# Gate and up products in two halves of the channels, in a layer with 32 experts

## The chip, the core and the metric

The kernel runs on one core of a Trainium2 chip. The metric is device time in microseconds (us), from three runs. The core's engines are TensorE (PE in the profile, PEld its weight loads), VectorE (DVE), ScalarE (ACT), GpSimd (POOL) and SyncE (SP), which here issues the weights' transfers.

## What is computed

One decoder block over 512 tokens of 1024 channels: a mixer (recurrent channels and windowed attention), then a mixture of 32 experts, in which each token goes to 4. The change touches the experts alone:

```
gu   = xb @ w_gu[e] + b_gu[e]                 # 1024 -> 2048
gate = minimum(gu[:, :1024], 7);  up = clip(gu[:, 1024:], -7, 7)
y    = ((up + 1) * gate * sigmoid(1.702 * gate)) @ w_down[e] + b_down[e]
out += router weight * y                       # rows of the tokens of expert e
```

With these inputs the experts get 48, 18, 90, 113, 36, 43, 293, 33, 22, 97, 64, 10, 23, 125, 10, 25, 113, 121, 13, 104, 39, 19, 3, 100, 68, 3, 42, 136, 69, 58, 17 and 93 rows (experts 0 to 31).

## The kernel before, in words

**Weights.** All is float32. An expert has eight chunks of gate and up weights (128 channels x 2048, 1 MB each) and four of down weights (1 MB). SyncE loads them in the order of use into a ring of 20 slots (`ORDER`, L1099). `pump` (L1129) issues loads as long as slots are free in program order; `paced` (L1105) makes SyncE read a word of the fourth load before, so that at most four are under way. `used` (L1134) gives back the slots of an expert's gate and up weights behind `gate_up`, those of its down weights behind `down`. A load into such a slot waits on the chip until TensorE has passed the last product that reads it, and with it the end of the nest of branches.

**Tiles.** The rows of an expert are taken in tiles of 32, up to four (a block of 128). `gu` (L1191) makes one tile's gate and up products: for each of 8 chunks (`k`) four products of 128x32 by 128x512, side by side in four column groups of the array, added up in one PSUM bank (`pg`, L1138). `act` (L1200) adds the bias and makes the activation: seven VectorE instructions and one on ScalarE, the result turned into `H[e % 2]`. `dn` (L1214) makes the tile's down products into half a bank (`pd`, L1140), and `put` (L1221) scales them on VectorE and adds them to their tokens' rows in HBM by an indirect DMA of GpSimd.

**Branches.** The tiles 1 to 3 stand in a nest of branches on the row count (`nest`, L1167): each engine falls through into a tile that exists, and jumps out behind the last one. `hint` tells an engine ahead of a tile whether the branch behind it will be taken. Experts with over 128 rows (6 and 27) run `further` (L1259) inside the innermost branch: blocks 1 to 3, each with gather, transposes, all products and sums. Its code stands in the instruction streams for every expert.

**Order.** One pass of the loop (L1303) for expert e: `gate_up(e)`, where two steps that prepare the row lists of expert e+2 (`prep`, `where`, `spots`) stand between pieces of tile 0; slots back; bias and transposes of the rows of expert e+1 (`turn_x`, `scale_x`) into the one buffer `xT`; the gather of the rows of e+2; `down(e-1)`; slots back. PSUM in this order: gate tiles 0 to 3 in banks 0 to 3, down tiles in banks 4 and 5 by turns, the transposes in 6 and 7, the lists in 5. In `further`: transposes in 0 and 1, gate tiles in 2 and 3, down tiles in 0 and 1. Block 1's rows are gathered into `XR` at the start of the pass (`second_rows`); the rows of block 2 and its lists ahead of block 1's products (L1272 to L1276).

Of the kernel before, what the change touches and what calls it, by code (L numbers as in the profile page):

```python
# [22 lines left out]
KD = 8  # L23
# [17 lines left out]
def block_kernel(ctx, tc, x, c, w_ada, b_ada, g_mix, w_in, conv_w, conv_b, w_rg_a, b_rg_a, w_rg_x,  # L41
# [16 lines left out]
    pall = psp.tile([128, 8, 512], FT, name="pall")  # L58
# [14 lines left out]
    class Carve:  # L73
# [3 lines left out]
        def tile(self, shape, dt, name=None, **kw):  # L77
            n = 1
            for d in shape[1:]:
                n *= d  # L80
            w = n if dt != BF else n // 2
            v = self.t[:shape[0], self.o:self.o + w]
            self.o += (w + 7) // 8 * 8
            assert self.o <= 2048, name
            v = v if dt == FT else v.bitcast(dt)
            if len(shape) == 3:
                v = v.rearrange("p (a b) -> p a b", a=shape[1])
            if len(shape) == 4:
                v = v.rearrange("p (a b c) -> p a b c", a=shape[1], b=shape[2])
            return v  # L90
# [639 lines left out]
    def run_all(g):  # L730
        for _ in g:
            pass
# [309 lines left out]
    def prep(e, c, oh, own=None, bk=5, tbs=range(NT)):  # L1042
        mk = (lambda n: own[n]) if own else new
        for tb in tbs:
            hot(oh, e, c, tb)
        yield
        where(e, c, oh, mk, bk)
        yield
        yield from spots(e, c, mk)
# [30 lines left out]
    def gather(e, b, x_, reg=None):  # L1080
        XROW[e, b] = x_

        def rows(p0, p1):
            G.indirect_dma_start(out=x_[p0:p1], out_offset=None, in_=h2_d,  # L1084
                                 in_offset=bass.IndirectOffsetOnAxis(
                                     ap=GI[e, b // 2][p0:p1, b % 2:b % 2 + 1], axis=0),
                                 bounds_check=S - 1, oob_is_err=False)

        if reg is None:
            return rows(0, 128)  # L1090
        with tc.If(reg > 128 * b + 64) as cmp:  # L1091
            rows(0, 128)
        with cmp.Else():
            with tc.If(reg > 128 * b + 32) as small:
                rows(0, 64)
            with small.Else():
                rows(0, 32)
# [33 lines left out]
            load(*todo.pop(0))  # L1131
            n = n and n - 1

    def used(e, down):  # L1134
        free.extend(HELD.pop((e, down)))
        pump()

    pg = lambda b, t: pall[:, 2 + t % 2 if b else t, :]  # L1138

    pd = lambda b, t: pall[:, (0 if b else 4) + t % 2, 0:256]  # L1140


    def xpose(e, b, xT):
        turn_x(e, b, xT)
        scale_x(e, b, xT, 0, 4)

    def scale_x(e, b, xT, k0, k1):
        p = pall[:, 0 if b else 6, :].rearrange("p (k n) -> p k n", k=4)
        for k in range(k0, k1):
            A.activation(xT[:, k, :], p[:, k, :], AF.Identity, scale=g2c[:, k:k + 1], bias=sh2c[:, k:k + 1])  # L1150

    def turn_x(e, b, xT):
        x_ = XROW[e, b]
        for q in range(2):
            p = pall[:, (0 if b else 6) + q, :].rearrange("p (k n) -> p k n", k=4)
            for i in range(4):
                k = 4 * q + i
                PE.transpose(p[:, i, :], x_[:, k * 128:(k + 1) * 128], ident)  # L1158
            if q:
                ks = slice(4, 8)  # L1160
                V.tensor_tensor(xT[:, ks, :], p, g2c[:, ks, None].to_broadcast([128, 4, 128]), op=OP.mult)
                V.tensor_tensor(xT[:, ks, :], xT[:, ks, :], sh2c[:, ks, None].to_broadcast([128, 4, 128]),
                                op=OP.add)
        XT[e, b] = xT


    def nest(r, b, body, after=None, mark=None):  # L1167
        with branch(r, 128 * b + 32, mark, 1):  # L1168
            hint(r, 128 * b + 64, mark, 2)
            body(1)  # L1170
            with branch(r, 128 * b + 64, mark, 2):  # L1171
                hint(r, 128 * b + 96, mark, 3)
                body(2)
                with branch(r, 128 * b + 96, mark, 3):
                    hint(r, 128 * b + 128, mark, 4, after)
                    body(3)
                    if after:
                        with branch(r, 128 * b + 128, mark, 4):
                            after()
# [7 lines left out]
    def hint(r, n, mark, i, there=True):  # L1187
        if mark and there:
            tc.mark_branch_hint_location(f"{mark}_{i}", hint=r > n, engines=WORKERS)

    def gu(e, b, t, k0=0, k1=KD):  # L1191
        xT, w = XT[e, b], WG[e]
        for k in range(k0, k1):
            for j in range(4):
                PE.matmul(pg(b, t)[32 * j:32 * j + 32], xT[:, k, 32 * t:32 * t + 32], w[k][:, j],  # L1195
                          start=(k == 0), stop=(k == KD - 1), tile_position=(0, 32 * j))
# [3 lines left out]
    def act(e, b, h, t):  # L1200
        p = pg(b, t)
        ga, up, sg, hr = (TU[:, i] for i in range(4))
        V.tensor_tensor(ga, p[:, 0:256], BG[:, 0:256], op=OP.add)  # L1203
        V.tensor_tensor(up, p[:, 256:512], BG[:, 256:512], op=OP.add)  # L1204
        V.tensor_scalar(ga, ga, 7.0, None, op0=OP.min)  # L1205
        A.activation(sg, ga, AF.Sigmoid, scale=1.702)  # L1206
        V.tensor_scalar(up, up, -7.0, 7.0, op0=OP.max, op1=OP.min)
        V.tensor_tensor(ga, ga, sg, op=OP.mult)  # L1208
        by_k = lambda v: v.rearrange("p (i k) -> p i k", k=KD)
        V.scalar_tensor_tensor(hr.rearrange("p (k i) -> p i k", k=KD), by_k(up), 1.0, by_k(ga),  # L1210
                               op0=OP.add, op1=OP.mult)
        V.transpose(h[:, t], hr)  # L1212
# [18 lines left out]


    H = [part(0), part(2)]
    TU, Y, HX, XR, bdx = part(1), part(3), part(4), a4[5], a4[6][:, :256]

    def gate_up(e, r, between):
        def tile(t):
            gu(e, 0, t)
            act(e, 0, H[e % 2], t)

        ks = (0, 2, 6, 8) if e else (0, 7, 8, 8)
        hint(r, 32, f"g{e}", 1)
        for i in range(3):
            gu(e, 0, 0, ks[i], ks[i + 1])
            if i < 2:
                between()
        act(e, 0, H[e % 2], 0)
        nest(r, 0, tile, lambda: further(e, r), f"g{e}")

    def down(e, r):  # L1250
        def tile(t):
# [7 lines left out]
    def further(e, r):  # L1259
        own = {n: new(n, n + "x") for n in ("g1", "i1", "gi", "f", "si")}  # L1260

        def products(t):
            gu(e, b, t)
            act(e, b, HX, t)

        def sums(t):
            dn(e, b, HX, t)
            put(e, b, t)

        def block():  # L1270
            xpose(e, b, XT[e, 0])
            if b < 3:  # L1272
                with tc.If(r > 128 * b + 128):
                    if b == 1:
                        run_all(prep(e, 1, T_HOT, own, 1))
                    gather(e, b + 1, XR)  # L1276
            products(0)
            nest(r, b, products)
            sums(0)
            nest(r, b, sums)  # L1280

        bias2(e, bdx)
        b = 1
        block()
        with tc.If(r > 256):
            b = 2
            block()
            with tc.If(r > 384):
                b = 3
                block()  # L1290

    pump(KD + 4 + EARLY)
# [10 lines left out]
    for e in range(NE):  # L1303
        r = rn
        if e:
            second_rows(e)
            bias2(e - 1)
        prs = [prep(e + 2, 0, T_HOT)] if e + 2 < NE else []
        if e == 0:
            prs = [prep(u, 0, OH[u], None, bk, ()) for u, bk in ((1, 5), (0, 7), (2, 4))]  # L1310
        for pr in prs:
            next(pr)
        if e == 0:
            gates_of()

        def between():
            for pr in prs:
                next(pr, None)
            if e == 0 and (1, 0) not in XROW:
                gather(1, 0, xg)  # L1320
                second_rows(0)

                nc.sync.value_load(xg.bitcast(I32)[0:1, 0:1])
                pump()

        gate_up(e, r, between)
        used(e, False)
        if e:
            hint(rp, 32, f"d{e - 1}", 1)
        for pr in prs:  # L1330
            run_all(pr)
        if e + 1 < NE:
            rn = count(e + 1)
            bias(e + 1)
            turn_x(e + 1, 0, new("xT"))
            scale_x(e + 1, 0, XT[e + 1, 0], 0, 4)
        if e + 2 < NE:
            gather(e + 2, 0, xg, G.value_load(cnt[0:1, e + 2:e + 3], min_val=0, max_val=S))  # L1338
        if e:
            down(e - 1, rp)  # L1340
            used(e - 1, True)
        rp = r
# [59 lines left out]
```

## Time and profile before

| | us |
|---|---|
| median of 3 runs | 1525.4 (1521.98 to 1530.1) |
| profiled execution | 1519.37 |
| its span, first to last instruction | 1517.5 |
| TensorE products, busy | 1226.6 |
| VectorE, ScalarE, GpSimd busy | 617.5, 210.3, 264.1 |
| mean granted clock of TensorE | 0.926 |

The span has a mixer part of some 250 us, the stage of the experts from about 257 to 1494 us, and a last norm. Products of 128x32 by 128x512 (L1195) run four at a time in the column groups, so a sum of their durations says nothing; a stretch in the timeline with its count does. In rows of waits, "<-" names what ended the wait, a small q behind an engine (PEq L1178) its sequencer: there, the exit of the nest at that line (L1168 behind one tile, L1171 two, L1174 three, L1178 four). L1288 and L1285 are the exits of `further`.

### The profile page before, as it was taken

How to read it: one execution, taken by the hardware profiler on the slowest of the kernel's cores; microseconds unless marked ns; L12 is line 12 of the kernel's file. 1: busy time of each engine (PE TensorE's matmuls, PEld its weight loads, DVE VectorE, ACT ScalarE, POOL GpSimd, SP SyncE). 2: the span in 40 equal slices, each digit the busy share in tenths (PEclk: the TensorE clock that was granted, in tenths of full speed). 3: DMA queues.
4: the chain of work that ended last, by engine and by line, in shares of the span. 5: the costliest groups of instructions: out<-in, count | busy, mean ns of one | idle time of the engine just before them, and what ended most of it. 6: DMA issues, size and time to landing. Idle time of an engine off the chain costs nothing. (4 is left out here: it accounts for less than half of the span.)

```text
span 1517.5 us, 32068 instructions
## 1 busy us (share of the span) xinstructions
PE 1226.6 (81%) x12297; PEld 541.8 (36%) x12297; DVE 617.5 (41%) x1687; ACT 210.3 (14%) x467; POOL 264.1 (17%) x224
## 2 busy tenths in 40 slices
PE   6998979678888988789777688798858887879782
PEld 4655657222332433223212322352412242233331
DVE  4738856424344333333323323433422343324323
ACT  3445524100100010000000000000000000000001
POOL 3305731100120012101100200110200031011102
PEclk9998999999999999989878988999978999999997
DMA  9973158897996039989998988897998899579963
GB/s 325 334 281 102 56 233 327 352 379 306 399 388 250 10 88 406 384 337 400 391 398 330 395 360 339 310 388 305 398 394 311 364 392 405 209 286 347 401 263 124
DMA packets 94319, 473.02 MB, mean 312 GB/s; under 512 B 12888, under 2 KB 36652, under 8 KB 42764
## 3 DMA queue, kind: packets, MB, share of 16 engines
q1 hardware_dynamic: 76684, 447.39, 74.5%
q0 software_dynamic: 16928, 20.21, 6.0%
q8 instruction: 176, 2.88, 0.8%
q14 instruction: 179, 1.47, 0.2%
q10 hardware_dynamic: 352, 1.07, 0.2%
HBM read 457.78 MB, written 17.06 MB: 313 GB/s over the span
## 5 line engine op out<-in xcount | busy, mean ns | idle before, releaser
L1195 PE MATMUL pall<-wc,xT 128*32 128x512 f32 x5248 | 643.0, 635 | 131.2 <-DMA wc<-in_w_gu_dram 64.4
L1195 PEld LDWEIGHTS pall<-wc,xT 128*32 128x32 f32 x5248 | 166.3, 114 | 526.1 <-issue 414.4
L1218 PE MATMUL pall<-wc,a 128*32 128x256 f32 x5248 | 306.2, 389 | 34.2 <-DVE a L1224 19.1
L1218 PEld LDWEIGHTS pall<-wc,a 128*32 128x32 f32 x5248 | 176.0, 112 | 157.5 <-issue 29.4
L1226 POOL DMA_INDIRECT x_d<-a,si x82 | 128.2, 1563 | 409.7 <-DVE a L1225 259.0
L1206 ACT ACTIVATE a<-a 128x256 f32<-128x256 f32 x82 | 34.2, 417 | 916.0 <-DVE a L1205 916.0
L1203 DVE TENSOR_TENSOR a<-pall,bg 128x256 f32<-128x256 f32 x82 | 34.8, 425 | 275.7 <-PE pall L1195 275.7
L1084 POOL DMA_INDIRECT xg<-h_d,gi x31 | 33.0, 1064 | 634.2 <-PE pall L1158 486.5
L1158 PE MATMUL pall<-ident,xg 128*128 128x128 f32 x248 | 37.7, 301 | 53.8 <-PEq L1168 23.4
L1150 ACT ACTIVATE xT<-pall,sh2c,g2c 128x128 f32<-128x128 f32 x136 | 51.2, 456 | 214.4 <-DVEq L1171 55.4
L1224 DVE TENSOR_TENSOR a<-pall,bd 128x256 f32<-128x256 f32 x75 | 31.7, 422 | 100.8 <-PE pall L1218 95.2
L928 DVE LOAD_MASK_SELECT bg<-btg x32 | 0.4, 14 | 155.2 <-DVEq L1171 48.5
L1056 DVE COPY f<-pall 128x8 f32<-128x8 f32 x33 | 5.5, 167 | 139.3 <-PE pall L1053 139.2
L1158 PEld LDWEIGHTS pall<-ident,xg 128*128 128x128 f32 x248 | 30.2, 154 | 81.1 <-issue 81.1
L1210 DVE SCALAR_TENSOR_TENSOR a<-a 128x256 f32<-128x256 f32 x82 | 50.1, 611 | 2.8
L233 PE MATMUL pall<-hp,wp 128*128 128x512 f32 x112 | 47.3, 422 | 2.3 <-ACT hp L287 1.7
L1208 DVE TENSOR_TENSOR a<-a 128x256 f32<-128x256 f32 x82 | 34.9, 426 | 27.9 <-ACT a L1206 23.5
L234 PE MATMUL pall<-hp,wp 128*128 128x512 f32 x112 | 45.3, 405 | 0.5 <-DVE hp L289 0.5
L235 PE MATMUL pall<-hp,wp 128*128 128x512 f32 x112 | 45.0, 402 | 0.0
L1225 DVE SCALAR_TENSOR_TENSOR a<-a,f,gt 128x256 f32<-128x256 f32 x82 | 39.7, 485 | 2.9
L1212 DVE STREAM_TRANSPOSE a<-a 128x256 f32<-128x256 f32 x82 | 36.5, 445 | 2.8
L1204 DVE TENSOR_TENSOR a<-pall,bg 128x256 f32<-128x256 f32 x82 | 34.0, 415 | 0.0
(295 smaller groups left out, 1015.3 us busy)
## 6 DMA issues: line engine op xcount, KB each, us to landing
wc<-in_w_gu_dram SPq DMA_DIRECT2D x256, 1024.0 KB, 11.1
wc<-in_w_down_dram SPq DMA_DIRECT2D x128, 1024.0 KB, 11.3
wc<-in_w_ada_dram SPq DMA_DIRECT2D x24, 1024.0 KB, 8.6
wc<-in_w_in_dram SPq DMA_DIRECT2D x7, 1024.0 KB, 11.9
a<-in_x_dram SPq DMA_DIRECT2D x4, 512.0 KB, 4.5
wc<-in_w_out_dram SPq DMA_DIRECT2D x4, 512.0 KB, 6.7
wc<-in_w_out_dram SPq DMA_DIRECT2D x2, 1024.0 KB, 4.8
out_dram<-wc SPq DMA_DIRECT2D x4, 512.0 KB, 2.7
```

What stands on the lines that cost most here:

```text
L233: PE.matmul(out, ah, bh, start=start, stop=False)
L234: PE.matmul(out, ah, bl, start=False, stop=False)
L235: PE.matmul(out, al, bh, start=False, stop=stop)
L1150: A.activation(xT[:, k, :], p[:, k, :], AF.Identity, scale=g2c[:, k:k + 1], bias=sh2c[:, k:k + 1])
L1158: PE.transpose(p[:, i, :], x_[:, k * 128:(k + 1) * 128], ident)
L1195: PE.matmul(pg(b, t)[32 * j:32 * j + 32], xT[:, k, 32 * t:32 * t + 32], w[k][:, j], start=(k == 0), stop=(k == KD - 1), tile_position=(0, ...
L1208: V.tensor_tensor(ga, ga, sg, op=OP.mult)
L1210: V.scalar_tensor_tensor(hr.rearrange("p (k i) -> p i k", k=KD), by_k(up), 1.0, by_k(ga), op0=OP.add, op1=OP.mult)
L1212: V.transpose(h[:, t], hr)
L1218: PE.matmul(pd(b, t)[32 * j:32 * j + 32], ht[:, t, 32 * k:32 * k + 32], w[k][:, j], start=(k == 0), stop=(k == KD - 1), tile_position=(0, ...
L1225: V.scalar_tensor_tensor(y, y, f[:, 1, b % 2, t:t + 1], gt2, op0=OP.mult, op1=OP.mult)
L1226: st = G.indirect_dma_start(out=x1_d, out_offset=bass.IndirectOffsetOnAxis(ap=si[:, b % 2, t:t + 1], axis=0), in_=y, in_offset=None, bound ...
```

## The change

`gate_up` runs the channels 0 to 511 (chunks 0 to 3) of all tiles first, in a nest of its own, then `further`, gives back the first four slots, and runs chunks 4 to 7 and the activation of all tiles in a second nest, whose exits have hints of their own; then the other four slots go back. The lists stand behind chunks 1 and 3 of tile 0. In `further` the banks are others, `xT` of the first block stays whole (`xt2` takes the turned rows of further blocks), `HX` and `XR` are one buffer, and the lists and the gather of block 2 (and the gather of block 3) stand behind the block before. The down products of the first block use banks 4 to 7.

```diff
-    def used(e, down):
-        free.extend(HELD.pop((e, down)))
+    def used(e, down, n=4):
+        free.extend(HELD[e, down][:n])
+        del HELD[e, down][:n]
         pump()
-    pg = lambda b, t: pall[:, 2 + t % 2 if b else t, :]
-    pd = lambda b, t: pall[:, (0 if b else 4) + t % 2, 0:256]
+    pg = lambda b, t: pall[:, 6 + t % 2 if b else t, :]
+    pd = lambda b, t: pall[:, 4 + (t % 2 if b else t), 0:256]
...
     def scale_x(e, b, xT, k0, k1):
-        p = pall[:, 0 if b else 6, :].rearrange("p (k n) -> p k n", k=4)
+        p = pall[:, 4 if b else 6, :].rearrange("p (k n) -> p k n", k=4)
...
-            p = pall[:, (0 if b else 6) + q, :].rearrange("p (k n) -> p k n", k=4)
+            p = pall[:, (4 if b else 6) + q, :].rearrange("p (k n) -> p k n", k=4)
...
-    TU, Y, HX, XR, bdx = part(1), part(3), part(4), a4[5], a4[6][:, :256]
+    TU, Y, HX, XR, bdx = part(1), part(3), part(5), a4[5], a4[6][:, :256]
+    xt2 = a4[4].rearrange("p (k n) -> p k n", k=KD)
     def gate_up(e, r, between):
+        hint(r, 32, f"g{e}", 1)
+        gu(e, 0, 0, 0, 2 if e else 4)
+        between()
+        gu(e, 0, 0, 2 if e else 4, 4)
+        between()
+        nest(r, 0, lambda t: gu(e, 0, t, 0, 4), lambda: further(e, r), f"g{e}")
+        used(e, False, 4)
+        hint(r, 32, f"h{e}", 1)
         def tile(t):
-            gu(e, 0, t)
+            gu(e, 0, t, 4, KD)
             act(e, 0, H[e % 2], t)
-        ks = (0, 2, 6, 8) if e else (0, 7, 8, 8)
-        hint(r, 32, f"g{e}", 1)
-        for i in range(3):
-            gu(e, 0, 0, ks[i], ks[i + 1])
-            if i < 2:
-                between()
-        act(e, 0, H[e % 2], 0)
-        nest(r, 0, tile, lambda: further(e, r), f"g{e}")
+        tile(0)
+        nest(r, 0, tile, None, f"h{e}")
+        used(e, False, 4)
...
         def block():
-            xpose(e, b, XT[e, 0])
-            if b < 3:
-                with tc.If(r > 128 * b + 128):
-                    if b == 1:
-                        run_all(prep(e, 1, T_HOT, own, 1))
-                    gather(e, b + 1, XR)
+            xpose(e, b, xt2)
             products(0)
...
         with tc.If(r > 256):
+            run_all(prep(e, 1, T_HOT, own, 4))
             b = 2
+            gather(e, b, XR)
             block()
...
         gate_up(e, r, between)
-        used(e, False)
```

## Rows read from the trace of the kernel before

**Rows 1.** The page of the profile: busy time of the engines, and the transfers' busy share in 40 slices of the span.
```profile
PE 1226.6 (81%) x12297; PEld 541.8 (36%) x12297; DVE 617.5 (41%) x1687; ACT 210.3 (14%) x467; POOL 264.1 (17%) x224
...
DMA  9973158897996039989998988897998899579963
```
**Rows 2.** The table by stretch: start and end us, us; busy us of TensorE, its weight loads, VectorE, ScalarE and GpSimd (instructions); granted clock; the transfers' share and GB/s.
```profile
1035.00:1174.00 139.00, 105.28 (x1092) 38.28 (x1090) 46.11 (x144) 9.24 (x24) 16.62 (x12) 0.89 0.96 376
...
1338.00:1475.00 137.00, 115.16 (x1330) 47.72 (x1330) 44.38 (x125) 9.36 (x24) 20.59 (x14) 0.95 0.93 358
```
**Rows 3.** SyncE's waits over the span: who waits, for what; us in total, times, longest.
```profile
SPq L1119 <- PEq L1288: 85.1, 1, 85.1
SPq L1119 <- PEq L1178: 74.7, 7, 13.5
SPq L1119 <- PEq L1285: 30.5, 1, 30.5
SPq L1119 <- PEq L1174: 21.8, 3, 8.8
```
**Rows 4.** The timeline of SyncE: start us, us from the first to the end of the last, what is issued, how many.
```profile
465.73 97.84 SPq L1119 DMA_DIRECT2D wc<-in_w_gu_dram  x8
...
1262.61 20.97 SPq L1119 DMA_DIRECT2D wc<-in_w_gu_dram  x8
...
1296.73 43.51 SPq L1119 DMA_DIRECT2D wc<-in_w_gu_dram  x8
```
**Rows 5.** TensorE's waits from 257 to 1494 us, columns as in group 3.
```profile
PE pall L1195 <- DMA wc<-in_w_gu_dram: 64.4, 45, 9.5
PE pall L1158 <- PEq L1168: 23.4, 11, 5.3
PE pall L1195 <- ACT xT L1150: 22.0, 6, 7.5
PE pall L1218 <- DVE a L1224: 19.1, 9, 2.4
PE pall L1195 <- PEq L1171: 13.5, 4, 4.5
...
PE pall L1158 <- PEq L1171: 8.7, 8, 1.7
PE pall L1158 <- PEq L1178: 7.3, 7, 1.1
...
PE pall L1158 <- PEq L1285: 6.2, 1, 6.2
PE pall L1158 <- PEq L1288: 5.2, 1, 5.2
...
PE pall L1158 <- PEq L1174: 3.1, 3, 1.0
```
**Rows 6.** The timeline of TensorE: start us, us, line, what it writes and reads, shapes, instructions (64 make a tile), and in brackets the wait before. The first row is gate tiles without a wait, the second two down tiles.
```profile
462.00 21.66 PE L1195 MATMUL pall<-wc,xT 128*32 128x512 f32 x200 [0.68 <-DMA wc<-in_w_gu_dram]
...
549.39 7.11 PE L1218 MATMUL pall<-wc,a 128*32 128x256 f32 x128 [0.45 <-PEq L1171]
```
**Rows 7.** The table by stretch, columns as in group 2, around four holes of the weight stream.
```profile
1020.00:1037.00 17.00, 15.98 (x164) 5.54 (x156) 7.92 (x21) 1.25 (x3) 0.87 (x1) 1.00 0.46 172
...
1303.00:1340.00 37.00, 26.77 (x272) 9.91 (x264) 13.57 (x36) 3.49 (x10) 1.57 (x1) 0.96 0.27 99
939.00:956.00 17.00, 16.12 (x152) 4.68 (x144) 6.07 (x17) 0.83 (x2) 0.00 (x0) 1.00 0.42 176
475.00:562.00 87.00, 76.56 (x879) 30.51 (x872) 32.32 (x88) 6.23 (x16) 10.44 (x7) 0.94 0.14 31
```
**Rows 8.** VectorE's waits over the span, for its own sequencer at the exit of the gate nest, ahead of the next expert's bias; columns as in group 3.
```profile
DVE bg L928 <- DVEq L1171: 48.5, 8, 6.4
DVE bg L928 <- DVEq L1178: 42.0, 7, 6.8
DVE bg L928 <- DVEq L1168: 41.0, 11, 5.8
DVE bg L928 <- DVEq L1174: 17.9, 3, 6.0
```
**Rows 9.** The timeline of VectorE: first and last of the seven instructions of one tile's activation.
```profile
374.91 0.42 DVE L1203 TENSOR_TENSOR a<-pall,bg 128x256 f32<-128x256 f32 x1 [3.82 <-PE pall L1195]
...
377.54 0.45 DVE L1212 STREAM_TRANSPOSE a<-a 128x256 f32<-128x256 f32 x1
```
**Rows 10.** Expert 6: the timeline of TensorE, block 1's transposes and its first products; that of GpSimd, the gather of block 2; and of the page's kind of list of DMA issues the row of such gathers (how many, median us from issue to landing).
```profile
483.60 1.09 PE L1158 MATMUL pall<-ident,small 128*128 128x128 f32 x8
...
490.48 29.52 PE L1195 MATMUL pall<-wc,xT 128*32 128x512 f32 x256 [0.16 <-issue]
...
490.74 1.04 POOL L1084 DMA_INDIRECT small<-h_d,gi  x1 [33.98 <-DVE f L1056]
...
xg<-h_d,gi POOLq DMA_INDIRECT x31, 8.1
```
**Rows 11.** The timeline of TensorE behind a wait (expert 10, tile 0), and the table by stretch for the time after it.
```profile
675.99 3.64 PE L1195 MATMUL pall<-wc,xT 128*32 128x512 f32 x16 [3.19 <-ACT xT L1150]
...
676.00:686.00 10.00, 9.43 (x52) 2.38 (x56) 4.53 (x15) 0.99 (x3) 1.57 (x1) 0.53 1.02 411
```

More of the change, by code (lines that the diff above doesn't have):

```diff
@@ L1289, in further @@
                 b = 3
+                gather(e, b, XR)
                 block()
```

## The prediction

> **What bounds the kernel now.** I read the page first. TensorE is busy for 81% of the span and the transfers' share by slices swings between 9 and 0 [rows 1], so neither limit holds throughout. The table by stretch says more: from 1035 to 1174 us the transfers run at a share of 0.96, from 1338 to 1475 at 0.93 [rows 2]. The expert stage therefore alternates: the weight stream is full for a while, then it stops, then TensorE waits for it. Why it stops is in SyncE's waits: 85.1 us in one wait for the exit of expert 6's further blocks, 30.5 us for expert 27's, and 74.7 and 21.8 us in ten waits for the exits of four- and three-tile experts [rows 3]. The ring has 20 one-megabyte slots. While expert e's gate and up products run, 12 are held and 8 can be filled; the next slots come free only behind the last tile. The timeline of SyncE shows the two largest holes: eight gate and up loads take 21.0 us to issue from 1262.61 us on, where none waits for a slot, but 97.8 us from 465.73 on and 43.5 from 1296.73 on [rows 4]. TensorE's waits show the other side: 64.4 us for gate and up weights, 22.0 for the turned rows xT, 19.1 for a bank that VectorE has not yet read, and 42.5 us (23.4 + 8.7 + 7.3 + 3.1) in 29 exits from the gate nest [rows 5].
>
> **Part 1, the split.** Multiplications, weight loads and bytes stay as they are. A gate tile costs 21.66 / 200 x 64 = 6.93 us, so a half 3.5 us; a down tile 7.11 / 2 = 3.56 us [rows 6]. New is that four slots come free after the first halves of all tiles, for a four-tile expert 13.9 us before the old point. The longest of the seven waits at such exits is 13.5 us [rows 3], so they nearly vanish; the four remaining slots follow 14 us later, about when four loads have landed. On SyncE the four loads move ahead of four others; behind them stand only loads, and nothing else uses that queue in this stage. Tile 0 now needs four chunks before the other tiles have work, not eight, so a starved start covers itself: three more half tiles (10.4 us) run while chunks 4 to 7 land. Of the 64.4 us of weight waits I take 40 as removed; the ends are 20 (the stream as late as now) and 64.
>
> How much room the stream has: its idle time is 17 x 0.58 = 10 us at 939 to 956, 17 x 0.54 = 9 at 1020 to 1037, 37 x 0.73 = 27 at 1303 to 1340, and 87 x 0.86 = 75 at 475 to 562 [rows 7]. The first two can go; of the third about 14 (half of four gate tiles earlier); of the fourth about 4, worked out in part 3; some 10 from smaller holes. Room: 47 us. A gain beyond that is not to be had from this edit.
>
> **Part 2, the exits.** Each nest is left by a jump. Today the gate nest's exit jumps over `further` as well, and costs TensorE 1.0 us where the hint stands a whole tile (7 us) ahead (7.3 / 7, 8.7 / 8, 3.1 / 3) but 5.2 and 6.2 us at the two exits of `further`, which have no hint [rows 5]. After the change the far jump closes the first half, with its hint only half a tile, 3.5 us, ahead. Bounds: 1.0 us each if the hint still suffices, 5.24 if it does nothing. Taken off 5.24, a lead of 3.5 us leaves 1.7; I take 2.0, nearer the lower row because that row's hint works the same way with a longer lead. For 30 experts (6 and 27 keep their price): 60 us. The second half gets an exit too, a short jump: 23 experts x 0.9 = 21 us, between 0 and the 3.4 us of 13.5 / 4, which are waits at short exits of the down nest [rows 5]; seven four-tile experts fall through. Against these stand the 42.5 us of today's exits. The net is +39.
>
> The Trainium skill, "Runtime: NRT & Kernel Launch", section "Instruction fetch mechanics", says that a taken branch to a target outside the fetched window stalls the engine until the target's page has come, and mentions no hint. The trace agrees for the two unhinted exits (5.2 and 6.2 us) and not for the hinted ones (1.0); by the rule alone the 60 us would be 157. What that does is the first rival.
>
> VectorE pays more at this exit: its bias shuffle waits 48.5 / 8 = 6.1, 42.0 / 7 = 6.0, 41.0 / 11 = 3.7 and 17.9 / 3 = 6.0 us behind it [rows 8]. Its part of a tile, 374.91 to 377.99, is 3.1 us [rows 9], less than the new 3.5 us per half tile, so it doesn't fall behind. VectorE meets the far jump while TensorE is still in the first halves, where it has nothing to do; from the second half it leaves by a short one. With two or more tiles the 6 us are hidden; with one tile VectorE starts its activation some 2 us late and then saves the jump, about even. So the turned rows of the next expert come some 4 us sooner after a large expert: four waits of 3.2 us, 13 of the 22.0. If the short jump stalls VectorE too, this is 0.
>
> **Part 3, banks and further blocks.** Four banks for down products, with VectorE no longer 6 us late, remove the 19.1 us. Banks 6 and 7 also hold the turned rows of the next expert; ScalarE and VectorE read them before down tile 2 comes, 7 us after the transposes. If VectorE is late as now, about half comes back (bounds 0 and 19).
>
> In expert 6 the lists and the gather of block 2 now stand after block 1 (XR and HX share a buffer). GpSimd's gather waits for the last reader of HX; behind it stand only block 2's scatters, and TensorE's transposes wait for it. Today the lists already cost TensorE the time from 484.69 to 490.48 us, 5.8 us, and the gather (1.04 us to issue, 8.1 to land) hides under block 1 [rows 10]. Then 9.1 us lie bare, bounds 5 and 20. The pause also lets the clock fall: after a wait of 3.19 us at 675.99 the next 10 us had 0.53 of the clock [rows 11], so I add 3.5. First release of slots for expert 6: half of four gate tiles (13.9 us) earlier, 9.1 later, so about 4 us sooner: that is the 4 above. Expert 27 has one block more than its first and no such gather.
>
> **The sum** on TensorE, against the profiled execution (span 1517.5, 1519.4 us in all): -40 -13 -19 +39 +9 +3.5 = -20.5. The stream has room for 47, so it permits that. Profiled time: 1499. The median of the runs, 1525.4, lies 6 us above the profiled one; against it I forecast 1504 us.
>
> **Rivals.**
> First, *the far jump decides, slower*. Place: TensorE's exit from the first half, 30 times. Price: 5.24 instead of 2.0, 97 us; pauses above 3 us also bring the low clock, as at 675.99 [rows 11], on perhaps ten of the 21 experts with several tiles, 3 us each. Against my 20.5 that is +107 if all lands on the path. It doesn't: with one tile the weight stream is the limit and covers it, so 21 x 3.2 + 30 - 20.5 = +77 at most. It decides from about 3 us per exit (21 x 1 us takes back my 20.5). For it: one-tile exits cost 2.1 us on average with a lead of a whole tile and up to 5.3 [rows 5], so hints fail at times. Against: all 18 hinted exits with two to four tiles cost about 1.0. All failing would give 1602. I take half as failing: 10.5 x 3.2 + 15 - 20.5 = +28, so 1553.
>
> Second, *the stream is the limit anyway, no change*. At shares of 0.96 [rows 2] earlier slots are filled no faster, the holes move to expert 6 and 27, and the rest eats what is left: 14 + 4 us at these two, less 3.5 of clock and about 10 of exits in large experts. Time: 1521. Against: the holes at 939 and 1020 us are of the kind that the earlier release ends.
>
> Third, *the exits stay at 1.0 us*, hints sufficing: another 30 us, held by the room of 47: 1480.
>
> Fourth, *VectorE's stall follows to the second exit*, so that the parts about turned rows and banks bring nothing: -20.5 + 13 + 10, 1528.
>
> **How the numbers follow.** A difference below 0.5%, 7.6 us, can't be told from none in this kernel. Forecast's own case 0.46 and range 1490 to 1516; third rival 0.10; first rival 0.28; second and fourth 0.16, of which a little falls on the faster side. Faster 0.57, same 0.15, slower 0.28. The range takes in the third rival and the first as far as half its exits failing: 1480 to 1552.
>
> **What would show it.** Right: SyncE's waits at exits of four-tile experts fall from 74.7 us to under 20, expert 6's wait stays above 70; TensorE's wait for gate and up weights about halves; its wait for VectorE's bank reads is gone; VectorE's 6 us waits move from the bias shuffle to the exit of the first half; TensorE shows 30 waits of about 2 us there; in expert 6 a pause of 12 to 18 us ahead of block 2. Wrong: waits of 3 us and more at the first exit in most experts with several tiles, with more stretches at the low clock; or the stream's holes at the old places.

## The result, and the profile after

| | us |
|---|---|
| before, median of 19 runs | 1524.57 |
| changed, median of 19 runs | 1536.28 (1528.72 to 1538.47) |
| ratio, 95% interval | 1.0068 [1.0053, 1.0084] |
| profiled execution, span | 1533.51, 1531.6 |

The change made the kernel slower by 0.7%. The prediction, 1504 us, had the sign wrong. Lines moved in the file: L1196 is the gate product (L1195 before), L1219 the down product, L1159 the transposes; nests are left at L1169 (one tile), L1172 (two), L1175 (three) and L1179 (four). L1292 and L1287 are the exits of `further`.

TensorE's waits from 257 to 1510 us in the changed kernel (who waits, for what; us in total, times, longest):
```profile
PE pall L1196 <- PEq L1169: 68.8, 15, 5.8
PE pall L1196 <- PEq L1172: 31.4, 11, 5.3
PE pall L1196 <- issue: 22.7, 10, 7.5
...
PE pall L1196 <- PEq L1179: 12.1, 7, 4.0
PE pall L1196 <- DMA wc<-in_w_gu_dram: 10.0, 2, 5.1
...
PE pall L1196 <- DMA wc<-in_w_down_dram: 8.2, 3, 2.8
...
PE pall L1196 <- ACT xT L1151: 1.2, 1, 1.2
...
PE pall L1219 <- DVE a L1225: 0.5, 1, 0.5
```
Against [rows 5], what was to go went, and more than was forecast: 64.4 us for weights are 10.0, 22.0 for turned rows are 1.2, 19.1 for banks 0.5. In its place stands TensorE's own sequencer, ahead of gate products. The timeline of expert 18 (one tile, no weights late) shows where: the first half ends at 995.3, the second begins at 1000.5.
```profile
993.41 1.92 PE L1196 MATMUL pall<-wc,xT 128*32 128x512 f32 x16
995.27 0.19 PE L1053 MATMUL pall<-g,rep 128*128 128x40 bf16 x1
1000.51 5.91 PE L1196 MATMUL pall<-wc,xT 128*32 128x512 f32 x32 [5.04 <-PEq L1169]
```
The second half then takes 5.91 us for 32 instructions where half a gate tile takes 3.5 [rows 6]: part of the pause is paid again in clock, of which 0.61 was granted there (the third figure from the end; columns as in [rows 2]):
```profile
1000.50:1006.40 5.90, 5.89 (x32) 1.35 (x32) 0.00 (x0) 0.00 (x0) 0.00 (x0) 0.61 0.98 378
```
VectorE's bias waits behind the exit, 149.4 us in [rows 8], are gone, as forecast:
```profile
DVE bg L928 <- DVEq L1169: 8.0, 11, 0.8
DVE bg L928 <- DVEq L1172: 7.5, 8, 1.0
...
DVE bg L928 <- DVEq L1175: 2.8, 3, 1.0
```
SyncE's waits for slots did not shrink but spread; at the exits of four-tile experts (L1179) 36.6 us are left of 74.7, where the prediction wanted under 20. They are no holes that starve anyone (TensorE's weight waits say so): SyncE waits for slots that a late TensorE still holds.
```profile
SPq L1119 <- PEq L1292: 86.8, 1, 86.8
SPq L1119 <- PEq L1172: 58.2, 11, 8.8
SPq L1123 <- PE pall L1196: 56.7, 27, 11.1
SPq L1119 <- PE pall L1219: 54.1, 21, 8.7
SPq L1119 <- PEq L1169: 41.2, 10, 7.1
SPq L1119 <- PEq L1175: 39.2, 6, 9.4
SPq L1119 <- PEq L1179: 36.6, 4, 11.9
SPq L1119 <- PEq L1287: 29.5, 1, 29.5
```
**A ledger of the stage.** The stage runs from the first gate product to the last down product. Its length, TensorE's waits over 0.3 us added up from the trace, and the time at half clock:

| kernel | stage | waits | at half clock |
|---|---|---|---|
| before | 1236.1 | 229.6 | 180.9 |
| changed | 1249.7 | 234.1 | 201.4 |
| split, no far jump | 1164.1 | 171.6 | 143.4 |
| before, no far jump | 1180.8 | 184.4 | 157.0 |

If half of the half-clock time counts as lost, the step from before to changed is 4.5 + 10.2 = 14.7 us, where the stage grew by 13.6. For the four kernels of the table the sum comes out within 5 us, so the experiments are read by TensorE's waits and clock. It isn't exact: against the kernel before, the later runs are off by up to 8 us, the first one with the far jump last by 36. And one profile is one execution: that of the kernel before had a granted clock of 0.926, 42 other runs of it 0.912 to 0.928, 0.919 on average, the 19 of the changed kernel 0.918. Over the runs the clock thus costs the change some 3 us, not 10.

### The profile page after: what moved, and what is told of

It reads as the page before. It is cut to its first block, busy times and chain, and to the rows that moved or that the text cites. A ratio compares the mean times of both kernels' runs of the same rounds, so it can differ in the third digit from the quotient of the medians.

```text
span 1531.6 us, 33030 instructions
## 1 busy us (share of the span) xinstructions
PE 1234.6 (81%) x12297; PEld 542.8 (35%) x12297; DVE 618.3 (40%) x1687; ACT 210.4 (14%) x467; POOL 263.3 (17%) x224
## 5 line engine op out<-in xcount | busy, mean ns | idle before, releaser
L1196 PE MATMUL pall<-wc,xT 128*32 128x512 f32 x4800 | 615.2, 654 | 184.2 <-PEq L1169 68.8
L1196 PEld LDWEIGHTS pall<-wc,xT 128*32 128x32 f32 x4800 | 162.8, 118 | 556.8 <-issue 534.1
L1219 PE MATMUL pall<-wc,a 128*32 128x256 f32 x4800 | 271.8, 384 | 9.1 <-issue 7.8
L1219 PEld LDWEIGHTS pall<-wc,a 128*32 128x32 f32 x4800 | 155.1, 111 | 116.8 <-issue 20.2
L1207 ACT ACTIVATE a<-a 128x256 f32<-128x256 f32 x82 | 34.2, 417 | 1039.3 <-DVE a L1206 1039.3
L1159 PE MATMUL pall<-ident,xg 128*128 128x128 f32 x248 | 34.1, 282 | 27.7 <-DVE a L1206 9.3
L1196 PE MATMUL pall<-wc,a 128*32 128x512 f32 x448 | 50.2, 607 | 0.2
L1151 ACT ACTIVATE xT<-pall,sh2c,g2c 128x128 f32<-128x128 f32 x124 | 46.7, 457 | 20.2 <-PE pall L1159 16.9
L1159 PEld LDWEIGHTS pall<-ident,xg 128*128 128x128 f32 x248 | 27.2, 143 | 54.9 <-DVE a L1206 16.3
L1073 DVE TENSOR_REDUCE i<-pall 128x2 f32<-128x4 f32 x33 | 5.4, 162 | 86.5 <-PE pall L1068 86.4
L1213 DVE STREAM_TRANSPOSE a<-a 128x256 f32<-128x256 f32 x75 | 33.4, 445 | 2.6
```

Source lines behind the costliest of these rows:

```text
L1219: PE.matmul(pd(b, t)[32 * j:32 * j + 32], ht[:, t, 32 * k:32 * k + 32], w[k][:, j], start=(k == 0), stop=(k == KD - 1), tile_position=(0, ...
```

## Experiments

The theory: the far jump over `further`, which now closes the first half, is taken before the code behind it has been fetched. Rivals: two nests cost more than one, whatever they jump over; the weight stream limits.

**No far jump.** In the split kernel and in the kernel before, `further` is emitted for experts 6 and 27 alone.
```diff
-... lambda: further(e, r), f"g{e}")
+... (lambda: further(e, r)) if e in (6, 27) else None, f"g{e}")
```


> The changed kernel, with the code of the further blocks emitted for experts 6 and 27 alone (with these inputs the only ones with over 128 rows). Theory 1, the far jump: TensorE waits 4.2 to 5.8 us behind the first half of one-tile experts, 2.2 to 2.6 at two tiles, because the jump over the further blocks has too little time for its code to come. Then these waits fall to 1 us or less in 30 experts, some 75 us on TensorE, and the time falls from 1536 to 1470 to 1490 us. Theory 2, the second nest as such (twice as many branches and exits, whatever their length): the waits stay at 2 us and more, 1525 to 1540 us. Theory 3, the weight stream has become the limit: the waits go but TensorE waits for weights instead, 1515 to 1535 us.

> The kernel before, with the further blocks emitted for experts 6 and 27 alone. Theory 1: here the far jump costs TensorE about 1 to 2 us per expert (42 us in all) and VectorE 6 us, which delay the turned rows (22 us) and the bank reads (19 us): without it 20 to 45 us less, 1480 to 1505 us. Then the split by itself is worth the difference to the run with the split. Theory 3, the holes of the weight stream hold the kernel before: 1515 to 1528 us.

Measured: split 1447.59 us (0.9483 [0.9465, 0.9501] of before), before 1470.63 (0.9637 [0.962, 0.9654]); both are below what I expected. The rivals fall. Code that is jumped over costs the changed kernel 89 us and the kernel before 55. Without it the split is worth 23 us; that this is near the forecast 20.5 is chance, since that sum held 39 us of exits. Expert 18 in the split without far jump, same rows as above:
```profile
940.35 1.92 PE L1196 MATMUL pall<-wc,xT 128*32 128x512 f32 x16
942.20 0.19 PE L1053 MATMUL pall<-g,rep 128*128 128x40 bf16 x1
942.78 3.64 PE L1196 MATMUL pall<-wc,xT 128*32 128x512 f32 x32 [0.39 <-DMA wc<-in_w_gu_dram]
```
The 5.0 us are gone and the products run at full clock. The transfers of instructions fall too, first the changed kernel, then the split without far jumps (queue; packets, MB, share):
```profile
q8 instruction: 199, 3.26, 0.8%
q14 instruction: 191, 1.56, 0.3%
```
```profile
q8 instruction: 163, 2.67, 0.7%
q14 instruction: 86, 0.70, 0.1%
```
That TensorE waits for code here, which the theory only argues, is seen in the times of these transfers. In the changed kernel 25 of the 30 first exits (all but experts 6 and 27) have a wait over 1 us, and in each a transfer of instructions on q8 (16 KB) ends 1.7 to 2.2 us before the next product; for expert 18 it is the one from 997.62 to 998.57 (the queue's row for 997.5 to 998.8 us):
```profile
q8 instruction: 1, 0.02, 4.6%
```
It begins 0.6 to 2.4 us after the last product at the eleven exits behind one tile, but before the last product's end at 11 of the 14 behind more. In the kernel before, each of VectorE's 24 long bias waits (5.6 to 6.8 us) has a transfer of instructions on q14 (8 KB) that ends 2.2 to 2.6 us before the wait does. Without far jumps two of the eleven one-tile exits (experts 22 and 25) still cost 5.1 and 4.2 us, each with a q8 transfer, so a short jump is not always cheap.

Mean wait of TensorE at the exit of the first half, by the expert's tiles (11, 8, 4 and 7 experts, 6 and 27 left out), read from the gap between its last and next gate product:

| kernel | 1 | 2 | 3 | 4 | sum, us |
|---|---|---|---|---|---|
| changed | 4.74 | 2.27 | 2.06 | 1.73 | 90.7 |
| no far jump | 1.29 | 0.85 | 0.74 | none | 22.6 |
| six chunks first | 3.58 | 0.97 | 2.26 | 1.05 | 63.4 |
| hint earlier | 4.60 | 2.22 | 2.29 | 1.40 | 87.3 |
| jump over one block | 4.13 | 2.83 | 2.68 | 0.77 | 84.1 |

Without the far jump these exits alone fall by 68 us (90.7 to 22.6). The last three rows belong to runs further below.

**Which engine, and how far.** Blocks 2 and 3 of `further` for expert 6 alone, in both kernels (in the kernel before also the lists and the gather that stand in block 1).
```diff
+        if e != 6:
+            return
         with tc.If(r > 256):
```


> The changed kernel, with the code of blocks 2 and 3 emitted for expert 6 alone, so that the jump of the other 30 experts passes one block: about a third of the way on TensorE, less on VectorE, which then also has no list code there. If any jump over more than TensorE has fetched costs the whole wait, its first exits stay at 4 to 5 us with one tile, 85 to 95 us in sum, and the time at 1520 to 1538 us. If the price goes with the distance, the sum falls to 30 to 60 us and the time to 1465 to 1510 us.

> The kernel before with the same cut: blocks 2 and 3 for expert 6 alone. TensorE's exits cost only about 1 to 2 us there anyway. If the 55 us that the far jump costs the kernel before are VectorE's 6 us waits, and one block is short enough for VectorE, these waits fall below 1 us and the time to 1470 to 1485 us, as without any far jump. If they are TensorE's, or one block is still too far, 1510 to 1528 us.

Measured: 1553.92 us (1.0192 [1.0162, 1.0222]) and 1491.29 (0.977 [0.9744, 0.9797]), the first outside both ranges, the second between them. In the kernel before, VectorE's waits ahead of the bias behind this nest are 1.0 us at most now, and 35 of its 55 us are gone while TensorE's exits cost what they did (44.3 us against 42.5):
```profile
DVE bg L928 <- DVEq L1168: 7.9, 10, 0.9
DVE bg L928 <- DVEq L1178: 6.6, 7, 1.0
DVE bg L928 <- DVEq L1171: 3.8, 4, 1.0
```
```profile
PE pall L1158 <- PEq L1168: 24.9, 12, 5.0
PE pall L1158 <- PEq L1171: 9.2, 8, 2.0
PE pall L1158 <- PEq L1178: 6.3, 6, 1.1
PE pall L1158 <- PEq L1174: 3.9, 3, 1.8
```
So there it was mostly VectorE's fetch, and one block is short enough for VectorE. TensorE's exits in the kernel before are hardly the far jump's at all: with no far jump those behind one to three tiles cost 34.2 us against 35.2.
```profile
PE pall L1158 <- PEq L1168: 23.0, 11, 5.1
PE pall L1158 <- PEq L1171: 8.0, 8, 1.1
PE pall L1158 <- PEq L1174: 3.2, 3, 1.1
```
In the split, one block is still too far for TensorE: the table shows nearly the old price, though three of the eleven one-tile exits cost 0.4 to 1.6 us. That the split got slower still, by 17.6 us, was in no expectation; its waits for which the profile names nobody doubled (30.3 to 60.5 us). Why, stays open.

**The lead of the hint.** Six chunks in the first part and two in the second:
```diff
-        gu(e, 0, 0, 2 if e else 4, 4)
+        gu(e, 0, 0, 2 if e else 4, 6)
...
-            gu(e, 0, t, 4, KD)
+            gu(e, 0, t, 6, KD)
```
(the first nest's tiles and the slots given back follow: six, then two) and, in another run, the first hint moved ahead of the down products:
```diff
-        hint(r, 32, f"g{e}", 1)
+        if not e:
+            hint(r, 32, f"g{e}", 1)
...
             scale_x(e + 1, 0, XT[e + 1, 0], 0, 4)
+            hint(rn, 32, f"g{e + 1}", 1)
```


> The changed kernel with six chunks in the first part and two in the second, so the far jump comes 5.2 us of products per tile behind the first hint, not 3.5. If the lead of the first hint sets the wait (one tile 4.7 us, two 2.3, three and four about 2 in the changed kernel; one tile with a whole tile's lead 2.1 in the kernel before): one tile 2.5 to 4 us, two tiles about 1, the sum of these exits from 90.7 to 45 to 65 us, the time 1490 to 1515 us. If the length of the first part doesn't matter: exits and time as in the changed kernel, 1528 to 1540 us.

> The changed kernel, with only the first hint of the far jump moved: ahead of the down products that come before, 3.6 to 14 us earlier on TensorE. If the lead of that hint sets the wait: one-tile exits from 4.7 to 1.5 us or less, two-tile ones to about 1, time 1475 to 1505 us. If another jump between hint and use (the exit of the down nest) undoes it: one-tile exits stay at 4 to 5 us, except perhaps behind four down tiles, where no jump stands between; 1525 to 1540 us.

Measured: 1517.22 us (0.9936 [0.9905, 0.9968]) and 1541.51 (1.011 [1.0062, 1.0158]). With six chunks, 1.7 us more of work per tile behind the hint took 1.2 us off the one-tile exits and the two-tile ones fell to 1.0; the time fell by 19 us, a little less than expected, and this version beats the kernel before by 0.6% with all its code in place. Further ahead, past the down nest, the hint gained nothing. The other jump alone doesn't explain it: behind four down tiles no jump stands between, and yet the six one-tile experts there (8, 11, 15, 18, 21 and 25) cost 4.9 to 5.6 us. Whether the down tiles' own hints do, or something else, stays open. So a longer first part helped, and a hint placed further ahead didn't.

**Far jump last.** `further` behind the second half, the second nest's hints from the expert's start, no hints on the first nest; then the same with the banks of the kernel before for `further`.
```diff
-        hint(r, 32, f"g{e}", 1)
+        hint(r, 32, f"h{e}", 1)
...
-        nest(r, 0, lambda t: gu(e, 0, t, 0, 4), lambda: further(e, r), f"g{e}")
+        nest(r, 0, lambda t: gu(e, 0, t, 0, 4))
...
-        nest(r, 0, tile, None, f"h{e}")
+        nest(r, 0, tile, lambda: further(e, r), f"h{e}")
```


> The changed kernel, with the further blocks behind the second half as in the kernel before, the first half's nest without hints, and the hints of the second nest from the start of the expert on (so a whole tile or more ahead of the far jump). Theory 1 with the lead as its cause: the first exit becomes a short jump, 1 us or less; the far one costs TensorE what it did before (1.0 us with several tiles, 1.3 to 5 with one); VectorE's 6 us wait comes back ahead of the bias. 1495 to 1515 us. Theory 2, two exits cost what they cost wherever the code lies: 1525 to 1540 us.

> As the run with the far jump last (1622 us), but the further blocks use the banks of the kernel before (0 to 3). There the transposes of the next expert waited 180 us for VectorE's sequencer at the exit; I put this down to banks 6 and 7, which further's gate tiles shared with these transposes. If so, these waits go, TensorE's exits cost about 1 us for the first half and 1 to 2 for the far one, VectorE's 6 us stand ahead of the bias as before: 1495 to 1515 us. If the order itself (VectorE's jump behind the second half) is what costs, over 1560 us.

Measured: 1622.05 us (1.0633 [1.0613, 1.0653]) and 1515.9 (0.9941 [0.9918, 0.9963]). The first was a surprise, and TensorE's waits over its span name it:
```profile
PE pall L1159 <- DVEq L1172: 61.2, 8, 8.5
PE pall L1159 <- DVEq L1179: 55.5, 7, 8.3
...
PE pall L1159 <- DVEq L1169: 37.8, 11, 3.8
PE pall L1159 <- DVEq L1175: 25.3, 3, 8.9
```
The next expert's transposes wait 180 us for VectorE to be through the exit, because `further` uses their banks 6 and 7: also where it isn't run, its readers are waited for at the exit. With other banks the rows are gone and the time is a little better than before. In both, the first exit, now a short jump without any hint, costs 0.5 us with two or three tiles, but with one tile 2.2 and 1.8 us on average: four of the eleven cost 2.9 to 5.5 us, the others 0.3 to 1.7. The expectation of 1 us or less doesn't hold there.

**What the split's 23 us are.** Both on the split without far jumps: all slots back together behind the second half; and tile 0 through all eight chunks first.
```diff
-        used(e, False, 4)
...
-        used(e, False, 4)
+        used(e, False, 8)
```
```diff
+        gu(e, 0, 0, 4, KD)
+        act(e, 0, H[e % 2], 0)
         nest(r, 0, lambda t: gu(e, 0, t, 0, 4), ...)
...
-        tile(0)
         nest(r, 0, tile, None, f"h{e}")
```


> The split without far jumps (further blocks for experts 6 and 27 alone, 1447.6 us), but all eight slots go back together behind the second half. If the earlier release is what the split is worth (1470.6 without the split, 1447.6 with it), the holes behind large experts and TensorE's waits for weights (6.9 us with it, 42 without the split) come back: 1462 to 1480 us. If the worth lies in the banks and in VectorE's order, 1443 to 1453 us.

> The split without far jumps (1447.6 us), but tile 0 goes through all eight chunks (and its activation) first; tiles 1 to 3 stay split and the slots go back where they did. Theory: the split is worth 23 us (1470.6 without it) because tile 0 needs only four chunks before other tiles have work; the early release is worth only some 4 us. Then TensorE's waits for gate and up weights come back from 7 us towards the 42 us without the split, 1458 to 1472 us. Rival: the worth lies in VectorE's order and the banks, 1444 to 1453 us.

Measured: 1451.9 us (0.95 [0.9459, 0.9541]), not told apart from the split's 0.9483; and 1464.8 (0.9598 [0.9574, 0.9622]), 17 us slower. Without the early release TensorE's waits for weights stay small:
```profile
PE pall L1196 <- DMA wc<-in_w_down_dram: 9.2, 3, 4.9
...
PE pall L1196 <- DMA wc<-in_w_gu_dram: 4.3, 7, 0.8
```
With tile 0 whole they come back in part, and one-tile experts leave two nests in a row:
```profile
PE pall L1159 <- PEq L1169: 33.4, 10, 4.5
...
PE pall L1196 <- DMA wc<-in_w_down_dram: 17.4, 6, 5.7
...
PE pall L1196 <- DMA wc<-in_w_gu_dram: 13.5, 13, 2.4
```
For comparison the split without far jumps:
```profile
PE pall L1196 <- DMA wc<-in_w_gu_dram: 6.9, 7, 3.4
PE pall L1196 <- DMA wc<-in_w_down_dram: 1.6, 2, 0.8
```
So the earlier slots show no gain of their own, and tile 0 in halves is worth 17 of the 23 us. What it saves is only in part waits for weights. They rise from 8.5 us to 31 (13.5 in the other run), while those for TensorE's own sequencer rise from 86.9 to 89.4 only; but about half of the 31, 16 us, are waits with an instruction transfer 1.7 to 2.4 us before their end, as at the exits above. Without such waits the rise is from 5 to 15 us. The other 6 of the 23 us were not looked for.

**Four banks alone**, in the kernel before:
```diff
-    pd = lambda b, t: pall[:, (0 if b else 4) + t % 2, 0:256]
+    pd = lambda b, t: pall[:, (t % 2 if b else 4 + t), 0:256]
```


> The kernel before with one part of the change alone: the down products of the first block in four banks (4 to 7). The prediction's part 3 says that TensorE's 19.1 us of waits for VectorE's bank reads go. If they lie on the path: 1505 to 1515 us. If the weight stream has slack behind them: 1518 to 1528 us, no difference.

Measured: 1522.52 us, 0.998 [0.9967, 0.9992]. TensorE's waits fell from 229.6 to 210.8 us, mostly the bank reads (19.1 to 2.3), but the stage stayed (1238.6 us): the time at half clock rose from 180.9 to 228.7. Part of this rise lies in the profile before with its high clock; over all runs the mean clock fell from 0.919 to 0.912, some 11 us. The waits for weights stayed as well (62.7 us). Why the clock took back what the waits gave is not shown.

## Why the prediction was wrong

**The step that failed** is the price of the far jump in part 2. It took the 5.24 us of an exit without a hint as the time that the code needs, took the lead of half a tile off it, and put 2.0 us on each of 30 exits, 60 in sum. Measured: 90.7. Behind two to four tiles the 2.0 us hold: the 19 exits cost 2.0 on average, 38.6 in sum. Behind one tile they don't: the eleven exits cost 4.7, nearly as if there were no hint, since the code's transfer begins only after the last product. There the hint stands ahead of tile 0, and from the start of that tile to the next product it takes about 10 us, not 5.2, however long the first part is: 4.8 + 4.7 in the changed kernel, 6.5 + 3.6 with six chunks, 8.5 + 2.1 in the kernel before (median lead, mean wait). That is an estimate from these three rows; the run with the hint further ahead doesn't follow it, and why the first hint does so much less than those inside the nest stays open. [rows 5] had a sign of it, 2.1 us on average at one-tile exits with a whole tile's lead, which I read as failures of the hint; they weren't the far jump's price, since they stayed without it (23.0 us). The second exits cost 27.7 us for 22 experts, forecast 21 (for 21 of them the profile names VectorE's activation, not TensorE's sequencer). Exits together rose by 76 us, not 39.

**The first rival** was the right one, and was priced too low in one place: I let the weight stream cover the one-tile exits. The split itself ended the lateness of the weights (64.4 to 10.0 us), and with that the cover; these exits are 52 of the 90.7 us. It also put the failures at the wrong exits, those with several tiles, and counted 21 of them where 30 less 11 are 19.

**The gains were right in kind.** Weights: forecast 40, measured 47 net of 7 us more behind down weights. It is rather more: all five waits left in the changed kernel (10.0 and 8.2 us) have an instruction transfer on q8 that ends 1.7 to 2.4 us before they do, and the two of 10.0 are one-tile exits (experts 12 and 22) that the 90.7 us count already. But the earlier release, on which part 1 spent its working of the holes, showed no gain that could be told from none; the order of halves did. Banks: the waits fell by 19 as forecast, though the run with the banks alone gained next to nothing by it. Turned rows: 21 us of waits went, forecast 13, but TensorE then stood at the exit of the down nest for its own code (41.2 us of such waits at the start of an expert, 23.3 before); all waits at the start of an expert fell only from 84.5 to 68.4 us. VectorE's 6 us were hidden, as forecast.

**Block 2 of expert 6** waited 7.8 us (524.84 to 532.62) where I expected 12 to 18, two more than before:
```profile
526.10 0.87 PE L1068 MATMUL pall<-vals,small 128*128 128x5 bf16 x8 [1.27 <-DVE small L951]
527.52 0.19 PE L1053 MATMUL pall<-g,rep 128*128 128x40 bf16 x1 [0.56 <-DVE g L1076]
532.62 1.94 PE L1159 MATMUL pall<-ident,small 128*128 128x128 f32 x8 [4.90 <-DMA small<-h_d,gi]
```
So the term of +9 was 2. The lists took 2.9 us here, 5.8 before. And I had taken the landing, 8.1 us, from the row of the 31 gathers into `xg`; gathers of this kind have a row of their own in the list of DMA issues before, with 4.3, and 4.3 us it took here:
```profile
small<-h_d,gi POOLq DMA_INDIRECT x3, 4.3
```

**Clock.** Forecast 3.5 us lost; in the two profiles the half-clock time rose by 20.5, so some 10, but over all runs the loss is some 3. So this term was about right.

**The rule set aside.** The Trainium skill ("Runtime: NRT & Kernel Launch", "Instruction fetch mechanics") says that a taken branch to a target outside the fetched window stalls the engine until the target has been fetched. I had set this aside for hinted exits. By the rule alone, at 5.24 us each, I had 157 us for these exits; measured were 90.7. So the hints are worth something behind several tiles (2.0 us), and the rule was nearer than my 2.0 behind one (4.7).

## What to carry to other kernels

Code that is jumped over had a price on both engines that were looked at, and it was paid where the jump stands: put it where the engine waits anyway, ask this for each engine by itself (here VectorE paid in the old place, TensorE in the new), and don't count on a hint: measure the wait behind it for each kind of exit, as a mean hides them (4.7 us behind one tile, 2.0 behind more). Waits for code can be told from others by the transfers of instructions just before their end. Before a wait is costed at what covers it, ask whether the change takes away that cover. And a part that isn't run can still be waited for: its banks and buffers tie others to the exit.

## What was not expected of the hardware

A jump over one block costs TensorE nearly as much as one over three (4.1 against 4.7 us with one tile), while VectorE's waits of 5.6 to 6.8 us are 1.0 at most at one block. In the kernel before, VectorE's hint stands one tile ahead (an estimate of 6.9 us, from the wait of 3.82 and the activation of 3.08 us in [rows 9]); all 18 waits behind several tiles were whole even so, and 6 of the 11 behind one, the other five 0.8 to 1.8 us. Short jumps of TensorE, over three half tiles, mostly cost 0.3 to 0.6 us, but up to 5 at times. And leaving out code that is never run, with every product in place, took 55 us (3.6%) off the kernel before and 89 us (5.8%) off the changed one. The fastest version of this study, 1447.59 us, is the split without far jumps; it holds for inputs in which no expert but 6 and 27 has more than 128 rows. Of those that keep all code, six chunks first (1517.22) and the far jump last with the old banks (1515.9) beat both kernels.
